# Gate tiles outside the ring, residual rows on GpSimd's queue, squares summed by additions, closing sums later

## The chip, the cores and the metric

The kernel runs on one core of one Trainium2 chip. The metric is the device time of one execution in microseconds (us); before the change the median of three executions is 1534.65 us.

## The reference

One decoder layer on x (256 positions x 2048 channels, float32), with 256 memory tokens:

```
x = x + hybrid_mixer(rms_norm(x, g1))          # w_in (five parts u, q, k, v, z and two logits per head), pooling, DeltaNet, w_mix_out
x = x + memory_cross_attention(rms_norm(x, g2), rms_norm(mem, gm))   # w_xq, w_xkv, w_xo
h = rms_norm(x, g3)
x = x + (silu(causal_dwconv(h @ w_gate) + b) * (h @ w_up)) @ w_down  # 2048 -> 5632 -> 2048
return rms_norm(x, g_final)
```

`rms_norm` multiplies by the reciprocal root of the mean square over the 2048 channels. Two of these norms matter here: the first (`rx`), whose squares are summed at the start, and the third (`r3`), whose sums close just before the gated MLP.

## The kernel before

Every weight is split into two float32r parts, a high part cast by ScalarE (ACT) and a low part, the difference, made by VectorE (DVE); a product is three matmuls on TensorE (PE): high by high, high by low, low by high. The programs of the engines are fixed when the kernel is built. Each engine runs its own in order, so an instruction that waits holds all that stand behind it on its engine; the DMAs that an engine issues stand in that same order.

**The start.** x arrives transposed. ACT squares it in four pieces of 128x1024 (L250) into `xsq`. The product with w_in runs head by head (`in_k`, casts and differences in lines 101 and 102). In between, `decays` works out the gates of the DeltaNet: `bc` and its transposes `lps`, then the sum of squares `xsum` by one TENSOR_REDUCE on DVE (L276, over the strided view of `xsq`), then `rnorm`, whose matmul `rxps` (L166) needs `xsum`, then a long chain of small DVE operations to `gg` (L304), the matmuls `gps` (L311) and the decay matmuls `dps` (L324).

**The gated MLP.** It begins where the last matmul of the cross-attention's output (`xo`, L141) ends. The gate and up weights are multiplied in 11 blocks of 22 steps, by a scheme of block sums and differences (seven products instead of eight). `plan` lists the steps: 11 kinds (`11`, `22`, `p1`, `s3`, `s1`, `p2`, `s2`, `21`, `p0`, `p3`, `s4`) of two tiles each, a tile being 128x1024. `load` (L987) fetches a tile 12 steps before its product, on SyncE's (SP's) queue; `prepare` splits it 4 steps before its product, and issues on GpSimd's (POOL's) queue the DMAs that add another weight onto a tile (L993) for the kinds built from sums. A first-gate tile (`11`) lies in `ring`, which is one of three large tiles under the tag "big" and takes the place of the attention's output `oT`; other tiles lie in 8 places under the tag "wr". The ring's tile is read again and again: by its own product, as target of L993 and L999, and as the source for `s1`, `s2` and `s4`.

**Beside the first block** two further jobs run, pumped along with the matmuls. `rows_of_x` turns the residual back to rows: 8 pieces of four PE transposes each (`xtp`), an ACT copy into `xt` (two places under the tag "sg") and a DMA to memory (`xspill`, L899, on SP's queue). `last_row` closes the sums of the third norm (`r3ps`, L166) and scales its last part. `xtp` and `r3ps` share the two PSUM banks under the tag "t".

Of the kernel before, what the change touches and what calls it, by code (L numbers as in the profile page):

```python
# [10 lines left out]
F32 = mybir.dt.float32  # L11
F32R = mybir.dt.float32r
AF = mybir.ActivationFunctionType
ALU = mybir.AluOpType
AX = mybir.AxisListType
NOSYNC = mybir.DependencyInfo(mybir.DependencyClass.NoSync, mybir.DependencyReason.DATA)

P = 128
# [24 lines left out]
def hybrid_trunk(ctx, tc, a, out):  # L43
    nc = tc.nc
    act, dve, pool, pe = nc.scalar, nc.vector, nc.gpsimd, nc.tensor
# [12 lines left out]
    def ev(name, n=T):  # L58
        return per.tile([P, n], F32, name=name, tag="ev", bufs=4)
# [4 lines left out]
    def job(lane, gen):  # L64
        lanes.setdefault(lane, []).append(gen)
# [15 lines left out]
    def drain(lane):  # L81
        while lanes.get(lane):
            advance(lane)
# [11 lines left out]
    def cv(k):  # L95
        s, e = CST[k]
        return cst[:, s:e]
# [15 lines left out]
    last_split = [None]  # L113
# [84 lines left out]
    with tc.tile_pool(name="dn", bufs=1, reuse_waits="tile") as dn:  # L198
# [18 lines left out]
        xsq = big("xsq", [P, KT, T], F32)  # L217
# [30 lines left out]
                    first(ps0, kt, hi[:, kt % 8, :], lo[:, kt % 8, :])  # L248
        for c in range(4):
            act.activation(xsq[:, c * 4:c * 4 + 4], xraw[c // 2][:, (c % 2) * 4:(c % 2) * 4 + 4], AF.Square)  # L250
        xsum = ev("xsum")
        nc.sync.dma_start(cst, a["cst"])
        rx, rxb, rxrun = rnorm([xsum], "rx")

# [10 lines left out]
        def decays():  # L265
            bc = dn.tile([16, T], F32, name="bc", tag="xp", bufs=3)
            act.copy(bc, bps[0:16, T:])
            dve.tensor_tensor(bc, bps[0:16, :T], bc, ALU.add)
            yield
            lps = pss.tile([P, 512], F32, name="lps", tag="s")  # L270
            for t in range(2):
                pe.transpose(lps[:, t * 16:(t + 1) * 16], bc[:, t * P:(t + 1) * P], cv("ident")[0:16, 0:16])
            lg = dn.tile([P, 2, 16], F32, name="lg")
            act.copy(lg.rearrange("p t c -> p (t c)"), lps[:, 0:32])
            with tc.issue_after(last_split[0].ins):
                dve.tensor_reduce(xsum, xsq.rearrange("p k t -> p t k"), AX.X, ALU.add)  # L276
            next(rxrun)
            yield from rxrun
            for t in range(2):
                dve.tensor_scalar(lg[:, t, :], lg[:, t, :], rx[:, t:t + 1], None, ALU.mult)  # L280
            blog = lg[:, :, 0:8].rearrange("p t h -> p h t")
            alog = lg[:, :, 8:16].rearrange("p t h -> p h t")
            act.activation(beta, blog, AF.Exp, scale=-1.0)
            dve.tensor_scalar(beta, beta, 1.0, None, ALU.add)
            dve.reciprocal(beta, beta)
            ea = dn.tile([P, 8], F32, name="ea")
            act.activation(ea, pv("a_log"), AF.Exp)
            xs, ab, yy, s1, s2, pp, gg = (sm(n) for n in ("xs", "ab", "yy", "s1", "s2", "pp", "gg"))
            dve.tensor_tensor(xs, alog, pv("dt_bias").unsqueeze(2).to_broadcast([P, HEADS, 2]), ALU.add)
            dve.tensor_scalar(ab, xs, -1.0, None, ALU.mult)  # L290
            dve.tensor_tensor(ab, ab, xs, ALU.min)
            act.activation(yy, ab, AF.Exp)
            dve.tensor_scalar(s1, yy, 2.0, None, ALU.add)
            dve.reciprocal(s1, s1)
            dve.tensor_tensor(s1, s1, yy, ALU.mult)
            dve.tensor_tensor(s2, s1, s1, ALU.mult)
            dve.tensor_scalar(pp, s2, 1.0 / 19.0, None, ALU.mult)
            for k in range(8, 0, -1):
                dve.scalar_tensor_tensor(pp, pp, 1.0 / (2 * k + 1), s2, ALU.add, ALU.mult)
            dve.scalar_tensor_tensor(pp, pp, 1.0, s1, ALU.add, ALU.mult)  # L300
            dve.tensor_scalar(xs, xs, 0.0, None, ALU.max)
            dve.scalar_tensor_tensor(xs, pp, 2.0, xs, ALU.mult, ALU.add)
            dve.tensor_scalar(ea, ea, -1.0, None, ALU.mult)
            dve.tensor_tensor(gg, xs, ea.unsqueeze(2).to_broadcast([P, HEADS, 2]), ALU.mult)  # L304
            ggf = fl(gg)
            mgr = dn.tile([P, P], F32R, name="mgr", tag="ktok", bufs=1)
            act.copy(mgr, cv("mgt"))
            for _ in range(7):
                yield
            gps = pss.tile([P, 512], F32, name="gps", tag="s")  # L310
            pe.matmul(gps[:, 0:16], cv("mle"), ggf, start=True, stop=True)  # L311
            pe.matmul(gps[:, 16:32], cv("mgt"), ggf, start=True, stop=True)
            act.activation(eg.rearrange("p s h t -> p (s h t)"), gps[:, 0:32], AF.Exp)
            dve.tensor_scalar(negA, egc, -1.0, None, ALU.mult)
            for q in range(4):
                gm = dn.tile([P, 4, P], F32, name="gm", tag="sq", bufs=1)
                for i in range(4):
                    dve.tensor_scalar(gm[:, i, :], cv("mle"), ggf[:, q * 4 + i:q * 4 + i + 1], None, ALU.mult)
                gh, gl = (dn.tile([P, 4, P], F32R, name=n, tag="C", bufs=2) for n in ("gh", "gl"))
                split(gh, gl, gm)  # L320
                yield
                yield
                dps = psd.tile([P, 512], F32, name="dps", tag="d")
                pe.matmul(dps, mgr, gh.rearrange("p i c -> p (i c)"), start=True, stop=False)  # L324
                pe.matmul(dps, mgr, gl.rearrange("p i c -> p (i c)"), start=False, stop=True)
                last_exp[0] = act.activation(Dm[q], dps.rearrange("p (i c) -> p i c", i=4), AF.Exp)
                pool.tensor_tensor(Dm[q], Dm[q], cv("mle").unsqueeze(1).to_broadcast([P, 4, P]), ALU.mult)
# [560 lines left out]
    acts = {}  # L888

    def rows_of_x():  # L890
        for q in range(8):
            t, n = q % 2, q // 2
            yield
            tp = pm.tile([P, 512], F32, name="xtp", tag="t", bufs=2)
            for i in range(4):
                pe.transpose(tp[:, half(i)], xres[:, 4 * n + i, half(t)], cv("ident"))
            xt = fp.tile([P, 512], F32, name="xt", tag="sg", bufs=2)
            act.copy(xt, tp)
            nc.sync.dma_start(xspill[t, :, n * 512:(n + 1) * 512], xt)  # L899
            yield  # L900


    latest = {}

    def seq(i):
        e = i.ins.engine
        if e in latest:
            tc.add_manual_dep(i.ins, latest[e], NOSYNC, reason="in the order of the text")
        latest[e] = i.ins.name
        return i  # L910
# [39 lines left out]
    def last_row():  # L950
        squared(15, sq3[0], "xo")
        scaled_rows(fp.tile([P, 1, T], F32, name="h15", tag="sg", bufs=2), 15, 1)
        r3, _, run = rnorm(sq3, "r3", False)
        job("r", run)
        return r3

    def parts(src, put=lambda i: i):
# [20 lines left out]
    def load(b, kind, j):  # L978
        w = {"11": 0, "22": 2, "21": 3, "s3": 1}.get(kind, int(kind[1]) if kind[0] == "p" else None)
        if w is None:  # L980
            return
        if kind == "11":
            r = ring[:, 2 * (b % 2) + j].rearrange("p (i c) -> p i c", i=2)
        else:
            r = fp.tile([P, 2, 512], F32, name="wr", tag="wr", bufs=8)
        raws[b, kind, j] = r
        nc.sync.dma_start(r, a["w_gu"][b, j, :, w])  # L987
# [44 lines left out]

    AHEAD, LOADS = 4, 8
    STAGES = (4, 6, 7, 8, 10, 12, 13, 15, 17, 18, 19, 21, 24, 25)
    job("xr", rows_of_x())
    convs = {}
    for s in range(LOADS):
        load(*plan[s])
    for s in range(-AHEAD, len(plan)):
        if s + LOADS + AHEAD < len(plan) and s + AHEAD >= 0:  # L1040
            load(*plan[s + LOADS + AHEAD])
        if s == -AHEAD:
            for q in range(LOADS, LOADS + AHEAD):
                load(*plan[q])
        if s + AHEAD < len(plan):
            prepare(*plan[s + AHEAD])
        if s == 1 - AHEAD:
            tc.add_manual_dep(added.ins, less[-1].ins.name, NOSYNC, reason="the last row's sums behind the first parts")
            with tc.issue_after(cast[-1].ins):
                r3 = last_row()  # L1050
        if s < 0:
            continue
        b, k = s // NS, s % NS
        if s == 16:
            drain("r")
        if k == 1 and b:
            convs[b - 1] = finish_block(b - 1)
        for c in (b - 1, b - 2):
            if c in convs and k + NS * (b - 1 - c) in STAGES:
                next(convs[c])  # L1060
        combine(b, k)
        multiply(*plan[s])
    for _ in convs[NB - 2]:
        pass
    job("cv", finish_block(NB - 1))
    drain("xr")


    arow = big("arow", [P, head_b, 4, T], F32)
# [35 lines left out]
    for m, (k, c) in enumerate(steps):  # L1105
# [4 lines left out]
        n = blocks.index(k // 4)  # L1110
# [122 lines left out]
```

## Time and profile before

| | |
|---|---|
| Median of three executions | 1534.65 us (1532.35 to 1535.73) |
| The profiled execution | 1533.36 us |
| Its span | 1531.6 us |
| Mean granted clock of TensorE | 0.992 |
| PE busy | 1490.8 us, 97% of the span |
| DVE busy | 1099.3 us, 72% |
| ACT busy | 856.4 us, 56% |
| POOL busy | 221.5 us, 14% |
| DMA | 314.95 MB, mean 206 GB/s |

The span is what the profiler sees between the first and the last instruction; the execution's own time is 1.8 us more. PE's 1490.8 us leave 41 us in which it has nothing to do. A granted clock below 1 in a stretch means that TensorE ran part of it at 1.2 GHz instead of 2.4 GHz. In a view of waits, each row names the waiting engine and line, what ended the wait, its total, how often, and the longest. The line numbers of the changed kernel are 2 higher in the start and 7 or 8 higher in the MLP.

### The profile page before, as it was taken

The page shows a single profiled execution, that of the slowest core. Times are in us where ns is not written, and L with a number is a line of the kernel's source. Part 1 is how long each engine was busy: PE and PEld are TensorE (multiplying, and loading weights), DVE is VectorE, ACT ScalarE, POOL GpSimd, SP SyncE. Part 2 cuts the span into 40 slices and gives each one's busy share as a digit, 9 for nine tenths or more (in the row PEclk, how much of TensorE's full clock was granted, in tenths as well). Part 3 has the DMA queues.
Part 4 walks back from the last instruction along what each step waited for, and adds up shares of the span by engine and source line. Part 5 has one row for each costly group of instructions (what it writes and reads, how often), then busy time and mean ns, then how long its engine had stood idle before and what let it go on. Part 6 is the DMA issues. An engine that isn't in the chain of part 4 may idle for free.

```text
span 1531.6 us, 20542 instructions
## 1 busy us (share of the span) xinstructions
PE 1490.8 (97%) x7722; PEld 1261.1 (82%) x7722; DVE 1099.3 (72%) x1435; ACT 856.4 (56%) x1247; POOL 221.5 (14%) x237
## 2 busy tenths in 40 slices
PE   7899999999999999999988999999999999999997
PEld 4788889888888888998877888888888888888885
DVE  6978887676544676666756898898999998455445
ACT  5555656554444544555545666666666666444433
POOL 0442532441100121000320000000000000000000
PEclk9999999999999999999999999999999999999999
DMA  6445443457555555344539888888888879755651
GB/s 225 155 176 176 151 170 126 141 173 268 190 176 190 192 191 192 138 140 163 193 129 339 248 256 261 260 256 268 269 270 242 244 217 365 249 194 191 197 188 55
DMA packets 73715, 314.95 MB, mean 206 GB/s; under 512 B 12048, under 2 KB 12432, under 8 KB 57488
## 3 DMA queue, kind: packets, MB, share of 16 engines
q1 hardware_dynamic: 67136, 290.05, 54.1%
q0 software_dynamic: 6336, 23.07, 8.4%
q8 instruction: 60, 0.98, 0.2%
q10 hardware_dynamic: 144, 0.52, 0.1%
q14 instruction: 39, 0.32, 0.1%
HBM read 304.05 MB, written 9.57 MB: 205 GB/s over the span
## 4 chain that ended last, share of the span: by engine, by line
PE 82%; DVE 7%; DMA 4%; ACT 2%; POOL 2%; issue 1%; SPq 1%; POOLq 0%; ACTq 0%; DVEq 0%
PE b L882 9%; PE b L884 9%; PE b L883 9%; PE acc L1096 5%; PE acc L1095 5%; PE acc L1094 5%; PE xq L143 4%; PE xo L143 4%; PE mix L143 4%; PE kk L143 3%; PE pvs L691 2%; PE pvs L690 2%; PE pvs L689 2%; PE xq L144 2%; PE xo L144 2%; PE mix L144 2%
## 5 line engine op out<-in xcount | busy, mean ns | idle before, releaser
L960 ACT CAST wh<-wr 128x1024 fp32r<-128x1024 f32 x154 | 160.2, 1050 | 82.4 <-DVE wr L996 30.0
L961 DVE TENSOR_TENSOR wl<-wr,wh 128x1024 fp32r<-128x1024 f32 x154 | 185.2, 1219 | 27.1 <-ACT wh L960 26.0
L882 PE MATMUL b<-wh,hP 128*128 128x512 f32 x484 | 192.4, 398 | 8.0 <-ACT wh L960 5.5
L884 PE MATMUL b<-wh,hP 128*128 128x512 f32 x484 | 191.8, 397 | 0.0
L883 PE MATMUL b<-wl,hP 128*128 128x512 f32 x484 | 190.6, 394 | 1.0 <-DVE wl L961 1.0
L961 DVE TENSOR_TENSOR wl<-wd,wh 128x1024 fp32r<-128x1024 f32 x88 | 107.5, 1224 | 101.9 <-ACT wh L960 100.3
L960 ACT CAST wh<-wd 128x1024 fp32r<-128x1024 f32 x88 | 92.7, 1054 | 118.5 <-PE acc L1096 115.7
L961 DVE TENSOR_TENSOR wl<-ring,wh 128x1024 fp32r<-128x1024 f32 x88 | 106.5, 1220 | 31.9 <-ACT wh L960 31.8
L960 ACT CAST wh<-ring 128x1024 fp32r<-128x1024 f32 x88 | 91.5, 1051 | 63.5 <-PE b L884 24.8
L1094 PE MATMUL acc<-wh,aring 128*128 128x512 f32 x320 | 124.5, 389 | 0.0
L1095 PE MATMUL acc<-wl,aring 128*128 128x512 f32 x320 | 124.5, 389 | 0.0
L1096 PE MATMUL acc<-wh,aring 128*128 128x512 f32 x320 | 124.5, 389 | 0.0
L882 PEld LDWEIGHTS b<-wh,hP 128*128 128x128 f32 x484 | 91.9, 190 | 28.0 <-ACT wh L960 5.8
L102 DVE TENSOR_TENSOR wil<-wi,wih 128x1024 fp32r<-128x1024 f32 x78 | 100.3, 1293 | 16.1 <-ACT wih L101 15.8
L883 PEld LDWEIGHTS b<-wl,hP 128*128 128x128 f32 x484 | 91.9, 190 | 20.3 <-DVE wl L961 1.9
L884 PEld LDWEIGHTS b<-wh,hP 128*128 128x128 f32 x484 | 91.8, 190 | 18.8
L993 POOL DMA_DIRECT2D ring<-in_w_gu x44 | 38.5, 879 | 422.2 <-DVE sg L932 343.1
L101 ACT CAST wih<-wi 128x1024 fp32r<-128x1024 f32 x78 | 81.4, 1048 | 18.0 <-DMA wi<-in_w_in 6.3
L143 PE MATMUL xq<-h2T,wqh 128*128 128x512 f32 x240 | 84.9, 393 | 0.0
L143 PE MATMUL kk<-mT,wkh 128*128 128x512 f32 x240 | 84.4, 393 | 0.0
L143 PE MATMUL xo<-oT,woh 128*128 128x512 f32 x240 | 84.3, 392 | 0.0
L143 PE MATMUL mix<-yT,wmh 128*128 128x512 f32 x240 | 84.1, 392 | 0.0
(466 smaller groups left out, 3769.9 us busy)
## 6 DMA issues: line engine op xcount, KB each, us to landing
wr<-in_w_gu SPq DMA_DIRECT2D x156, 512.0 KB, 7.0
wd<-in_w_down SPq DMA_DIRECT2D x88, 512.0 KB, 4.8
wi<-in_w_in SPq DMA_DIRECT2D x39, 1024.0 KB, 5.0
ring<-in_w_gu POOLq DMA_DIRECT2D x44, 512.0 KB, 7.4
wk<-in_w_k SPq DMA_DIRECT2D x16, 1024.0 KB, 4.9
wv<-in_w_v SPq DMA_DIRECT2D x16, 1024.0 KB, 4.8
wm<-in_w_mix SPq DMA_DIRECT2D x16, 1024.0 KB, 4.9
wq<-in_w_xq SPq DMA_DIRECT2D x16, 1024.0 KB, 4.9
```

Source lines behind the costliest of these rows:

```text
L101: act.copy(hi, src)
L102: return dve.tensor_tensor(lo, src, hi.bitcast(F32), ALU.subtract)
L143: pe.matmul(ps, h, full, start=kk == 0, stop=False)
L144: i = pe.matmul(ps[:, T:], l, xt[:, 0, :], start=False, stop=False)
L882: pe.matmul(ps, xh, wh, start=first and i == 0, stop=False, skip_group_check=True)
L883: pe.matmul(ps, xh, wl, start=False, stop=False, skip_group_check=True)
L884: m = pe.matmul(ps, xl, wh, start=False, stop=last and i == 1, skip_group_check=True)
L960: cast[:] = [put(act.copy(h, src))]
L961: less[:] = [put(dve.tensor_tensor(l, src, h.bitcast(F32), ALU.subtract))]
L1094: pe.matmul(acc[t, n], ah, wh, start=first, stop=False)
L1095: pe.matmul(acc[t, n], ah, wl, start=False, stop=False)
L1096: return pe.matmul(acc[t, n], al, wh, start=False, stop=last)
```

## The change

Four parts:

1. The two `11` tiles of the first block go to the "wr" places; those of later blocks stay in the ring.
2. The 8 residual rows are copied to four places of a tile of their own (tag "ac"), leave by POOL's queue, and are advanced by a written step (`next(leaving)`) in steps 3 to 19 of block 0, no longer pumped.
3. The squares are summed by five additions, issued right behind the squares; the TENSOR_REDUCE is gone.
4. `last_row` yields six times more before it closes its sums.

```diff
             act.activation(xsq[:, c * 4:c * 4 + 4], xraw[c // 2][...], AF.Square)
+        for c in range(1, 4):
+            dve.tensor_tensor(xsq[:, 0:4], xsq[:, 0:4], xsq[:, 4 * c:4 * c + 4], ALU.add)
+        dve.tensor_tensor(xsq[:, 0:2], xsq[:, 0:2], xsq[:, 2:4], ALU.add)
         xsum = ev("xsum")
+        dve.tensor_tensor(xsum, xsq[:, 0], xsq[:, 1], ALU.add)
...
-            with tc.issue_after(last_split[0].ins):
-                dve.tensor_reduce(xsum, xsq.rearrange("p k t -> p t k"), AX.X, ALU.add)
...
     def rows_of_x():
+        rows = fp.tile([P, 4, 512], F32, name="xt", tag="ac", bufs=1)
         for q in range(8):
             t, n = q % 2, q // 2
             yield
             tp = pm.tile([P, 512], F32, name="xtp", tag="t", bufs=2)
             for i in range(4):
-                pe.transpose(tp[:, half(i)], xres[:, 4 * n + i, half(t)], cv("ident"))
-            xt = fp.tile([P, 512], F32, name="xt", tag="sg", bufs=2)
-            act.copy(xt, tp)
-            nc.sync.dma_start(xspill[t, :, n * 512:(n + 1) * 512], xt)
+                seq(pe.transpose(tp[:, half(i)], xres[:, 4 * n + i, half(t)], cv("ident")))
             yield
+            seq(act.copy(rows[:, q % 4], tp))
+            nc.gpsimd.dma_start(xspill[t, :, n * 512:(n + 1) * 512], rows[:, q % 4])
...
-        job("r", run)
+        def later():
+            for _ in range(6):
+                yield
+            yield from run
+
+        job("r", later())
...
-        if kind == "11":
+        if kind == "11" and b:
             r = ring[:, 2 * (b % 2) + j].rearrange("p (i c) -> p i c", i=2)
         else:
             r = fp.tile([P, 2, 512], F32, name="wr", tag="wr", bufs=8)
...
-    job("xr", rows_of_x())
+    leaving = rows_of_x()
...
+        if 3 <= s < 20:
+            next(leaving, None)
...
-    drain("xr")
```

At the start, DVE's program changes as follows, behind the products' first differences (`w0l`; `wil` are the differences of the weights in_w_in):

```order
 L106 SCALAR_TENSOR_TENSOR hT<-xraw,prm,hT 128x256 x8
 L102 TENSOR_TENSOR w0l<-w_79,w0h 128x1024
-L268 TENSOR_TENSOR bc<-bps,bc 16x256
-L102 TENSOR_TENSOR wil<-wi,wih 128x1024 x2
-L276 TENSOR_REDUCE xsum<-xsq 128x256
-L102 TENSOR_TENSOR wil<-wi,wih 128x1024
+L252 TENSOR_TENSOR xsq<-xsq 128x1024 x2
+L272 TENSOR_TENSOR bc<-bps,bc 16x256
+L252 TENSOR_TENSOR xsq<-xsq 128x1024
+L253 TENSOR_TENSOR xsq<-xsq 128x512
+L255 TENSOR_TENSOR xsum<-xsq 128x256
+L102 TENSOR_TENSOR wil<-wi,wih 128x1024 x4
```

The reduction stood between the second and the third difference; the additions now stand ahead of the first difference, two of them also ahead of `bc`.

On SP, the loads from the last one of the cross-attention (`wo`) on, before:

```order
L110 DMA wo<-in_w_xo 128x2048 x16
L987 DMA ring<-in_w_gu 128x1024 x2
L987 DMA wr<-in_w_gu 128x1024 x10
L899 DMA xspill<-xt 128x512
L987 DMA wr<-in_w_gu 128x1024 x2
L899 DMA xspill<-xt 128x512
L987 DMA wr<-in_w_gu 128x1024
L899 DMA xspill<-xt 128x512
L987 DMA wr<-in_w_gu 128x1024
```

and now:

```order
L110 DMA wo<-in_w_xo 128x2048 x16
L994 DMA wr<-in_w_gu 128x1024 x9
L994 DMA ring<-in_w_gu 128x1024
L994 DMA wr<-in_w_gu 128x1024 x5
L994 DMA ring<-in_w_gu 128x1024
L994 DMA wr<-in_w_gu 128x1024 x4
L994 DMA ring<-in_w_gu 128x1024
```

The ring no longer stands first: nine loads into "wr" places stand ahead of it, and the residual rows have left this queue.

On POOL, the same stretch before (`sq` are the squares of the third norm, `r3r` its reciprocal root):

```order
L716 TENSOR_TENSOR sq_6743<-sq_6743,xos 128x256 x7
L993 DMA ring<-in_w_gu 128x1024 x2
L716 TENSOR_TENSOR sq_6743<-sq_6743,xos 128x256
L172 TENSOR_TENSOR r3r<-r3ms,cst 128x2
L993 DMA ring<-in_w_gu 128x1024 x42
```

and now:

```order
L718 TENSOR_TENSOR sq_6747<-sq_6747,xos 128x256 x7
L1000 DMA wr<-in_w_gu 128x1024 x2
L718 TENSOR_TENSOR sq_6747<-sq_6747,xos 128x256
L902 DMA xspill<-xt 128x512
L172 TENSOR_TENSOR r3r<-r3ms,cst 128x2
L902 DMA xspill<-xt 128x512
L1000 DMA wr<-in_w_gu 128x1024 x2
L902 DMA xspill<-xt 128x512 x5
L1000 DMA ring<-in_w_gu 128x1024
L902 DMA xspill<-xt 128x512
L1000 DMA ring<-in_w_gu 128x1024 x39
```

The eight rows now stand among the accumulating DMAs: two ahead of the second pair, seven ahead of the first one for block 1, all eight ahead of the next.

## Rows read from the trace of the kernel before

**Rows 1.** TensorE's waits in the whole span: engine, line, releaser, total, times, longest.

```profile
PE b L882 <- ACT wh L960: 5.5, 1, 5.5
PE dps L324 <- ACT gh L101: 2.7, 3, 1.8
...
PE b L882 <- DVE ring L1019: 2.5, 1, 2.5
PE gps L311 <- DVE gg L304: 1.9, 1, 1.9
...
PE xtp L896 <- ACT xt L898: 1.7, 1, 1.7
PE in_k L144 <- DVE wil L102: 1.2, 2, 0.8
...
PE rxps L166 <- DVE xsum L276: 0.8, 1, 0.8
```

**Rows 2.** Busy us of each engine, granted clock, DMA share and GB/s by stretch.

```profile
35.00:39.00 4.00, 4.00 (x16) 3.41 (x15) 2.64 (x3) 0.48 (x1) 0.93 (x1) 0.60 0.61 199
60.00:72.00 12.00, 10.13 (x53) 7.96 (x52) 12.00 (x23) 6.47 (x11) 7.62 (x7) 1.00 0.46 164
773.00:791.00 18.00, 18.00 (x106) 15.81 (x105) 8.67 (x12) 6.34 (x11) 3.48 (x3) 1.00 0.00 1
791.00:797.00 6.00, 0.50 (x4) 0.19 (x2) 0.13 (x1) 1.04 (x1) 0.00 (x0) 0.91 0.71 237
797.00:803.00 6.00, 5.53 (x13) 3.70 (x13) 5.28 (x6) 4.88 (x7) 3.03 (x3) 0.52 0.99 357
803.00:808.00 5.00, 3.81 (x21) 2.95 (x20) 3.92 (x4) 2.40 (x5) 0.00 (x0) 1.00 1.04 283
808.00:852.00 44.00, 40.58 (x183) 32.82 (x184) 29.24 (x28) 25.22 (x31) 5.13 (x5) 0.96 1.02 350
852.00:900.00 48.00, 48.00 (x221) 39.66 (x220) 42.48 (x46) 32.69 (x39) 3.46 (x4) 1.00 0.83 235
900.00:1200.00 300.00, 300.00 (x1378) 246.84 (x1376) 270.88 (x296) 198.44 (x232) 24.39 (x28) 1.00 0.87 258
1240.00:1500.00 260.00, 260.00 (x1164) 215.09 (x1163) 152.95 (x145) 124.38 (x130) 1.74 (x2) 1.00 0.67 223
```

**Rows 3.** DVE's timeline at the start: start, us, engine, line, what, [idle before].

```profile
16.64 1.22 DVE L102 TENSOR_TENSOR w0l<-w,w0h 128x1024 fp32r<-128x1024 f32 x1
19.93 0.41 DVE L268 TENSOR_TENSOR bc<-bps,bc 16x256 f32<-16x256 f32 x1 [2.07 <-ACT bc L267]
23.32 2.36 DVE L102 TENSOR_TENSOR wil<-wi,wih 128x1024 fp32r<-128x1024 f32 x2 [2.98 <-ACT wih L101]
25.59 7.44 DVE L276 TENSOR_REDUCE xsum<-xsq 128x256 f32<-128x4096 f32 x1
32.94 1.22 DVE L102 TENSOR_TENSOR wil<-wi,wih 128x1024 fp32r<-128x1024 f32 x1
```

**Rows 4.** Of the tile ring's instructions: durations min/median/max in ns, first and last start.

```profile
L1019 DVE TENSOR_TENSOR ring<-q,b x11: 686/686/689, 838.3 to 1266.9; 128x512 f32<-128x512 f32 x11
...
L993 POOL DMA_DIRECT2D ring<-in_w_gu x44: 857/868/1060, 798.7 to 1259.7; - x44
```

**Rows 5.** SP's queue's waits for xo and for the rows' copies, 785 to 900 us.

```profile
SPq L987 <- PE xo L141: 25.0, 1, 25.0
SPq L899 <- ACT xt L898: 14.5, 6, 3.3
```

**Rows 6.** DVE's timeline ahead of the MLP: the last two parts of hP.

```profile
772.13 1.23 DVE L102 TENSOR_TENSOR hP<-hc,hP 128x1024 fp32r<-128x1024 f32 x1 [0.57 <-ACT hP L101]
...
788.56 0.96 DVE L102 TENSOR_TENSOR hP<-hc,hP 128x768 fp32r<-128x768 f32 x1 [1.81 <-ACT hP L101]
```

**Rows 7.** ACT's timeline at the first cast of the MLP.

```profile
795.79 1.04 ACT L960 CAST wh<-ring 128x1024 fp32r<-128x1024 f32 x1 [7.26 <-DMA ring<-in_w_gu]
```

**Rows 8.** ACT's waits for the residual rows' landing, 785 to 860 us.

```profile
ACT xt L898 <- DMA xspill<-xt: 8.8, 5, 2.7
```

## The prediction

> **What bounds the kernel now.** I read the shares of the span first: TensorE is busy for 1490.8 of 1531.6 us, so no more than about 41 us can be had without taking matmuls away, and this change, which takes none away, can only act on TensorE's pauses and on its clock. So I read next TensorE's own waits over the whole span [rows 1], to see where the pauses lie, and then the busy time, clock and DMA share by stretch [rows 2], to see what is around them. Two places belong to this change. At the start (20 to 75 us) TensorE waits for xsum, for a difference (wil), for gg and for gh, in sum 6.6 us [rows 1], and between 35 and 39 us it works at a granted clock of 0.60 [rows 2]. At the beginning of the MLP (791 to 852 us) it waits 5.5 us for the first cast, 1.7 us at the row transposes and 2.5 us for a combination in DVE [rows 1], and its clock is 0.52 from 797 to 803 us [rows 2]. Behind 852 us it is busy for all of 48, 300 and 260 us in the three stretches shown [rows 2]: what is won before that is not lost to a wait that is there already, and reaches the end unless loads, casts or differences fall behind.
>
> **The squares.** Removed: one reduction of 7.44 us on DVE, which starts at 25.59 [rows 3]. Added: three additions of 128x1024 at 1.22 us (a difference of that shape, the row of 16.64), one of 128x512 at 0.69 [rows 4] and one of 128x256 at 0.41 (the addition of bc, which has as many elements in a lane) [rows 3]: 3 x 1.22 + 0.69 + 0.41 = 4.76 us. They stand ahead of the first difference, where DVE is idle for 2.07 us ahead of bc and 2.98 us behind it, 5.05 us in all [rows 3]. So I cost them at nothing; what hides them are DVE's waits for bc and for the cast of wih. If that cover were gone they would cost 4.76 us, still 2.7 less than the reduction. xsum is then there near 22.7 us instead of 33.0, and the third difference, at 32.94 behind the reduction, follows the first two at once.
>
> What TensorE gets of it. (a) 0.8 us of waiting for xsum and about 0.4 of the wil row's 1.2 (its longest wait, 0.8, lies ahead of the reduction and stays). (b) The low clock of 35 to 39 us follows that pause; work at a granted share of 0.60 for 4.00 us loses 4.00 x 0.40 = 1.6 us [rows 2]. (c) The waits for gg (1.9) and gh (2.7) [rows 1] end a chain on DVE that starts from the norm's factor, and so from xsum. That chain starts some 7 us earlier, but on an engine that is full: 12.00 of 12 us from 60 to 72 [rows 2]. Bounds: nothing of (c), since DVE's work is not less by more than 7.44 - 4.76 us and TensorE comes earlier too, against all 4.6 us. The additions lie in idle time, so DVE's own row moves up by the full 7.44 while TensorE moves up by 2.8; that is nearer to the upper end, and I take 3.2. Sum of the start: 0.8 + 0.4 + 1.6 + 3.2 = 6.0 us, with ends at 2.8 and 7.4.
>
> **First gate tiles.** Before, SP's first MLP load waits for the last matmul of xo, 25.0 us [rows 5], since the ring takes the place of oT; everything behind it on that queue waits too. From 773 to 791 us the DMA engines are idle (share 0.00, 1 GB/s) [rows 2]. The first cast starts at 795.79, after 7.26 us in which ACT waited for that tile [rows 7]. Now nine loads into "wr" places stand ahead of the ring's first. By the places' former users the first seven need nothing later than the part of hP of 772.13, which ends at 773.4; the eighth needs the last part, 788.56 to 789.5 [rows 6]. So seven tiles (7 x 0.524 = 3.67 MB) come between 773 and 791, in idle DMA time, and the first casts and differences follow ACT's and DVE's last work for hP, before TensorE ends xo at 791.4. TensorE does not stop, and with the pause its low clock goes.
>
> What is there to be won, by stretch [rows 2]: idle 5.50 + 0.47 + 1.19 + 3.42 = 10.6 us from 791 to 852 us, and lost to the clock 5.53 x 0.48 + 40.58 x 0.04 = 2.65 + 1.62 = 4.3 us: 14.9 us, the upper end.
>
> What limits it is the DMA. From 797 to 852 us its share is 0.99 to 1.04 [rows 2]. The bytes from 791 to 852 are 6 x 237 + 6 x 357 + 5 x 283 + 44 x 350 kB = 20.4 MB, and the 55 full us move 345 GB/s. Take away the 3.67 MB that now come early, let the rest start at 789.5 with the eighth load, and the same point of the program is reached at 789.5 + 16.7 / 0.345 = 837.9 at the full rate, and at 839.8 if only the last xo matmul releases the bulk. That is 14.1 or 12.2 us before 852. I take 12.5, near the second, since two pauses can remain inside: the transposes wait for an ACT copy that stands behind casts (1.7 now, [rows 1]), and the combination in DVE that TensorE waited 2.5 us for stands where it stood. With both of them kept and coming on top it would be 12.2 - 4.2 = 8.0, the lower end.
>
> **Rows and closing sums.** The eight row DMAs leave SP's queue, where they stood between loads, and ACT's 8.8 us of waiting for their landing [rows 8] goes with the four places. They are issued by POOL at the price of a DMA there, 0.87 us (857 to 1060 ns) [rows 4]: 8 x 0.87 = 7.0 us on an engine that is busy for 5.1 of 44 us [rows 2]. Each stands ahead of accumulating DMAs and holds these until its ACT copy is done. I cost this at nothing beyond the two pauses above; what hides it is that an accumulation is issued four steps ahead of its product, and a step is (61 - 15) / 22 = 2.1 us of TensorE, so 8 us of cover. Without the cover, all 7.0 us would show. The bytes are the same, so the sum of the DMA stands. The later closing sums take matmuls from behind step 3 to behind step 5 and wait for POOL's last square no longer; nothing needs their result before the scaling of step 16: nothing either way.
>
> *A rule against this part.* The row's issues on POOL took at most 1060 ns, though DVE was busy for 270.88 of the 300 us in which most of them fall. The Trainium skill, "DMA: Bandwidth & Descriptors", section "SWDGE vs HWDGE vs iDMA", advises plain transfers on SP or ACT, since descriptors that GpSimd writes are held up by some of DVE's instructions; "SBUF — State Buffer", section "A bandwidth-pool intuition that's wrong", gives some 3100 ns where 620 was normal, a factor of 5. By the row the rows cost 7.0 us of hidden issue time; by the rule 35, which would not be hidden.
>
> **Sum.** -6.0 - 12.5 = -18.5 us on the profiled execution's 1533.4: 1514.9. The median of the runs shown is 1.3 above the profiled one, so 1516 us.
>
> **Rivals.**
> - *The start gives back.* DVE, full from 60 to 72 us, sets the start whatever TensorE does, and only the MLP pays, with nothing to 2.8 us from the start: 1534.65 - 12.5 - 1.4 = 1521 us. For it: the 12.00 of 12. Against it: 7.44 us leave DVE itself.
> - *The early tiles gain little.* If the loads of 773 us wait after all for something late, or the DMA is what counts and the bulk starts at 791.4 as before, then 20.4 MB / 0.345 = 59 us end at 850.5: 2 us of gain instead of 12.5, and with the start 1534.65 - 2 - 6 = 1527 us. For it: DMA shares of 1.0 up to 852. Against it: idle DMA from 773 on, and a wait [rows 5] that names xo alone.
> - *POOL's queue holds up the sums (slower).* The row issues stand in order with the accumulations, seven of them ahead of block 1's first, and each waits for its ACT copy, as SP did at most 3.3 us for one [rows 5]. If these waits don't lie beside each other, a row takes 0.87 + 3.3 = 4.2 us of the queue, the accumulation behind all eight comes 33.4 us later, 8 are covered, and TensorE stops for 25.4 us in block 1 and restarts at the low clock (2.65, as at 797 us): 1516 + 28 = 1544 us, slower than before. Up to 1.0 us a row it does nothing; the kernel is as slow as before from 3.0 us a row (24 - 8 + 2.65 = 18.65). Against it: a row comes only every second step, 4.2 us, so POOL is done with one before the next, and the longest of 44 issues took 1.06 us. (By the Trainium skill's factor, above, the issue alone would take 4.35 us, beyond the point from which this decides; the trace's 1.06 speaks against it.)
>
> **How the numbers follow.** A measurement of this kernel can tell about 0.2%, 3 us, from no change. Forecast with both gains 0.64 (own range 1510 to 1521); start given back 0.12; early tiles gain little 0.12; POOL's queue 0.05; the remaining 0.07 for what no row shows, half of it near no change. Faster takes the first three less a little: 0.87; same 0.06; slower 0.07. The range reaches from the upper ends of both sums (1534.65 - 7.4 - 14.9 = 1512, less 2 for what a profile's spread can hide, 1510) to the second rival's 1527.
>
> **What would show it.** In the profile after: no reduction on DVE, TensorE's wait for xsum gone and the clock near 1.0 from 30 to 39 us; waits for gg and gh below 2 us in sum; loads landing from 773 us on; the first MLP product within 1 us of the last xo matmul, at full clock; no wait for a landing at the copies of the rows; POOL's row issues near 0.9 us; TensorE's idle time over 791 to 840 us below 3 us. The forecast is wrong if TensorE stops again between steps 3 and 21 for an accumulation or a load, or if the DMA's full stretch ends no earlier than before.

## The result and the profile after

The changed kernel takes 1518.61 us (median of four executions, 1517.98 to 1519.94); its ratio to the kernel before is 0.9899, 95% interval 0.9881 to 0.9916, so 15.5 us less (12.9 to 18.3). The forecast was 1516, its range 1510 to 1527. The profiled execution took 1517.98 us, with a span of 1516.2.

TensorE's waits over the whole span of the changed kernel, to be set beside [rows 1] (engine, line, releaser, total, times, longest):

```profile
PE gps L313 <- DVE gg L306: 3.0, 1, 3.0
PE dps L326 <- ACT gh L101: 2.8, 2, 2.5
PE xtp L899 <- ACT xt L901: 2.4, 2, 1.5
...
PE in_k L143 <- ACT wih L101: 1.4, 1, 1.4
PE b L884 <- DVE ring L1026: 1.1, 1, 1.1
PE in_k L144 <- DVE wil L102: 0.8, 1, 0.8
```

The 5.5 us for the first cast of the MLP are gone, and so is the wait for xsum. But gg is now waited for 3.0 us instead of 1.9, and gh 2.8 instead of 2.7. The stretches of [rows 2], after (busy us of each engine, granted clock, DMA share, GB/s):

```profile
35.00:39.00 4.00, 4.00 (x23) 3.15 (x22) 3.77 (x11) 1.80 (x5) 1.39 (x1) 1.00 0.51 215
48.00:60.00 12.00, 10.47 (x51) 9.07 (x52) 10.22 (x23) 6.27 (x11) 4.14 (x4) 0.86 0.25 89
60.00:72.00 12.00, 9.14 (x44) 7.10 (x44) 10.84 (x20) 6.58 (x11) 6.93 (x7) 0.94 0.34 107
72.00:80.00 8.00, 8.00 (x47) 7.16 (x46) 6.01 (x8) 6.98 (x16) 4.05 (x6) 0.87 0.61 233
773.00:791.00 18.00, 18.00 (x100) 15.60 (x99) 10.39 (x13) 9.94 (x14) 5.36 (x6) 1.00 0.65 213
791.00:797.00 6.00, 6.00 (x30) 4.99 (x29) 5.84 (x6) 3.23 (x5) 0.00 (x0) 1.00 1.01 260
797.00:803.00 6.00, 4.50 (x25) 3.77 (x25) 3.91 (x5) 3.12 (x5) 1.32 (x2) 1.00 0.78 271
803.00:808.00 5.00, 4.08 (x22) 3.09 (x21) 3.16 (x3) 2.93 (x4) 0.05 (x1) 1.00 0.97 338
808.00:852.00 44.00, 42.89 (x202) 35.02 (x201) 34.45 (x33) 28.81 (x36) 7.47 (x11) 1.00 0.94 313
852.00:900.00 48.00, 48.00 (x221) 39.57 (x221) 43.92 (x50) 32.46 (x38) 4.36 (x5) 1.00 0.89 259
```

The low clock of 35 to 39 us is gone, but two others have come, from 50 to 54 and from 71 to 74 us, behind the waits for gg and gh. From 773 to 900 us the clock is 1.00 in all the stretches, and 10.6 us of idle time have become 3.5 (1.50 + 0.92 + 1.11; the prediction's sign asked for less than 3). On SP the first nine loads are issued from 769 us on (seven by 773 us, the eighth at 785, the ninth at 792), and ACT's first casts of the MLP stand directly behind its part of hP of 128x768; first SP's timeline, then ACT's:

```profile
769.03 23.70 SPq L994 DMA_DIRECT2D wr<-in_w_gu  x9
```

```profile
783.28 0.83 ACT L101 CAST hP<-hc 128x768 fp32r<-128x768 f32 x1
784.02 3.90 ACT L967 CAST wh<-wr 128x1024 fp32r<-128x1024 f32 x4
```

**Two marks.** From the traces I take two times of each kernel: the start of TensorE's last xo matmul (what lies before it is the start's gain), and the time from there to the first transpose of the gate, gt (22 steps of block 0 and the first of block 1; in every kernel the same number of matmuls). Before: 791.0 and 66.8 us. After: 786.6 and 54.9 us. So in this pair of profiles 4.4 us come from ahead of the MLP and 11.9 from its beginning; behind gt both kernels take nearly the same, 422 us to the down projection's first matmul and 241 to 242 from there to its last; the changed one loses 0.9 us there, all in all, which makes the 15.4 us between the two spans.

| kernel | last xo | xo to gt | timed median | ratio to before (95%) |
|---|---|---|---|---|
| before | 791.0 | 66.8 | 1534.7 | 1 |
| changed | 786.6 | 54.9 | 1518.6 | 0.9899 (0.9881 to 0.9916) |
| changed, again | 788.7 | 53.1 | 1519.3 | 0.9904 (0.9884 to 0.9924) |
| additions alone | 788.2 | 66.7 | 1533.5 | 0.9998 (0.9988 to 1.0008) |
| gate tiles alone | 793.0 | 66.8 | 1531.5 | 0.9981 (0.9970 to 0.9993) |
| changed, old rows | 788.7 | 66.8 | 1529.2 | 0.9973 (0.9962 to 0.9983) |
| changed, tiles in the ring | 789.7 | 64.0 | 1527.9 | 0.9958 (0.9942 to 0.9973) |
| changed, two places | 788.6 | 64.1 | 1527.3 | 0.9956 (0.9939 to 0.9972) |
| changed, rows pumped | 786.9 | 61.8 | 1524.7 | 0.9935 (0.9915 to 0.9955) |
| changed, with the reduction | 791.8 | 52.5 | 1521.8 | 0.9921 (0.9905 to 0.9937) |
| changed, sums not later | 788.4 | 54.0 | 1519.7 | 0.9910 (0.9891 to 0.9928) |
| changed, rows on SP | 787.5 | 52.3 | 1516.7 | 0.9889 (0.9875 to 0.9904) |
| the same, no double load | 787.9 | 52.4 | 1517.6 | 0.9889 (0.9873 to 0.9905) |
| changed, gps later | 794.0 | 52.4 | 1521.8 | 0.9925 (0.9910 to 0.9940) |

The first two columns are of one profiled execution each, the others of the timed ones; I compare kernels by their ratios, since each ratio is taken to the kernel before as it ran beside it.

### The profile page after: what moved, and what is told of

Its sections match the earlier page's. It is cut to its first block, busy times and chain, and to the rows that moved or that the text cites. A ratio compares the mean times of both kernels' runs of the same rounds, so it can differ in the third digit from the quotient of the medians.

```text
span 1516.2 us, 20536 instructions
## 1 busy us (share of the span) xinstructions
PE 1483.5 (98%) x7722; PEld 1257.2 (83%) x7722; DVE 1097.7 (72%) x1439; ACT 856.9 (57%) x1247; POOL 224.7 (15%) x245
## 4 chain that ended last, share of the span: by engine, by line
PE 82%; DVE 6%; DMA 4%; ACT 3%; POOL 2%; issue 2%; SPq 0%; DVEq 0%; POOLq 0%; ACTq 0%
PE b L884 9%; PE b L886 9%; PE b L885 9%; PE acc L1102 5%; PE acc L1103 5%; PE acc L1104 5%; PE xq L143 4%; PE mix L143 4%; PE xo L143 3%; PE kk L143 3%; PE pvs L693 2%; PE pvs L692 2%; PE pvs L691 2%; PE xq L144 2%; PE mix L144 2%
## 5 line engine op out<-in xcount | busy, mean ns | idle before, releaser
L967 ACT CAST wh<-wr 128x1024 fp32r<-128x1024 f32 x162 | 168.4, 1050 | 90.8 <-PE b L886 32.0
L968 DVE TENSOR_TENSOR wl<-wr,wh 128x1024 fp32r<-128x1024 f32 x162 | 194.8, 1219 | 29.4 <-ACT wh L967 28.0
L967 ACT CAST wh<-ring 128x1024 fp32r<-128x1024 f32 x80 | 83.2, 1051 | 52.8 <-PE b L886 26.9
L968 DVE TENSOR_TENSOR wl<-ring,wh 128x1024 fp32r<-128x1024 f32 x80 | 96.7, 1218 | 20.1 <-ACT wh L967 20.1
L1000 POOL DMA_DIRECT2D ring<-in_w_gu x40 | 34.9, 872 | 378.8 <-DVE sg L934 350.8
```

What stands on the lines that cost most here:

```text
L967: cast[:] = [put(act.copy(h, src))]
L968: less[:] = [put(dve.tensor_tensor(l, src, h.bitcast(F32), ALU.subtract))]
```

## The experiments

**The additions alone**, in the kernel before:

```diff
+        for c in range(1, 4):
+            dve.tensor_tensor(xsq[:, 0:4], xsq[:, 0:4], xsq[:, 4 * c:4 * c + 4], ALU.add)
+        dve.tensor_tensor(xsq[:, 0:2], xsq[:, 0:2], xsq[:, 2:4], ALU.add)
+        dve.tensor_tensor(xsum, xsq[:, 0], xsq[:, 1], ALU.add)
-                dve.tensor_reduce(xsum, xsq.rearrange("p k t -> p t k"), AX.X, ALU.add)
```

> The kernel before with the additions alone in place of the reduction. Theory: all that the start gives comes from the additions; of the 5.2 us that TensorE is ahead at the end of its fourth unit (42.11 instead of 47.32 us) 4.4 are lost again at gps, which now stands 12 matmuls earlier and waits 2.98 us for gg, with a stretch at 1.2 GHz behind it; 0.8 us are left at 78 us, and 3.2 more come between 140 and 160 us, where the stretch at 1.2 GHz at 154 us is gone: 1534.7 - 4.0 = 1530.7 us, the same waits for gg (about 3.0) and gh (about 2.8) as in the changed kernel. Rival: the 3.2 us at 150 us belong to the chance of one execution, not to the additions: 1533.8 us. Second rival: without the MLP's part the start keeps its 6.0 us, as predicted: 1528.7 us.

Measured: 1533.46 us, ratio 0.9998; 0.3 us less, at most 1.8. The first rival's time came nearest, 1533.8; the theory's 4.0 us and the predicted 6.0 are excluded by the interval. The waits are those of the theory, though (gg 3.0, gh 2.6), and this kernel's profile has its last xo matmul 2.8 us earlier than before. That profiled execution was the shortest of the ten, 1530.5 us.

**The reduction back**, in the changed kernel (the additions out, the TENSOR_REDUCE in):

```diff
-        for c in range(1, 4):
-            dve.tensor_tensor(xsq[:, 0:4], xsq[:, 0:4], xsq[:, 4 * c:4 * c + 4], ALU.add)
...
+                dve.tensor_reduce(xsum, xsq.rearrange("p k t -> p t k"), AX.X, ALU.add)
```

> The changed kernel with the single reduction of the squares back in place of the additions. Theory: the additions give nothing that lasts, since gps and dps come earlier and wait longer (alone they gave 0.5 us, interval -1.2 to 1.8): within 1.5 us of the changed kernel, in whose first 80 us the reduction's wait (0.8) and the stretch at 1.2 GHz near 35 us come back and the wait for gg falls from 3.0 to 1.9. Rival: the profiles are right, by which the additions put TensorE 2 to 4 us ahead behind 160 us: 2 to 4 us more than the changed kernel.

Measured: ratio 0.9921 against 0.9904 of the changed kernel beside it, 2.6 us more: the rival's size (2 to 4), not the theory's (within 1.5), but with intervals that overlap. One stretch of its start shows the old picture again:

```profile
31.00:39.00 8.00, 6.86 (x23) 5.95 (x24) 5.49 (x7) 1.09 (x2) 1.61 (x1) 0.57 0.49 166
```

All ten profiles with the additions and gps in its place have the last xo matmul between 786.6 and 789.7 us, the three without them between 791.0 and 793.0. So profiles say some 3 to 4 us, the timed runs 0.3 to 2.6. What part of the 15.5 us the additions give stays open between 0 and 4; none of these numbers reaches the 6.0 of the prediction.

**gps later**, in the changed kernel:

```diff
-            for _ in range(7):
+            for _ in range(9):
                 yield
             gps = pss.tile([P, 512], F32, name="gps", tag="s")
```

> The changed kernel with nine yields instead of seven ahead of gps, which puts gps 9 matmuls later on TensorE and the four dps pairs 9, 15, 19 and 20 matmuls later. Theory: the start gave back its gain because gps and dps stand too early for DVE's chain; now gps waits about 1.5 us instead of 3.0, the last dps not at all instead of 2.5, and at least one of the two stretches at 1.2 GHz (50.1 and 70.6 us, 1.7 us each) goes: 4 to 6 us less, 1512.6 to 1514.6 us. Rival: DVE's chain sets the pace there, the waits only move on to qp and w behind 140 us: 1518.6 us, within 1 us, with the wait for Z longer than 1.6 us.

Measured: 1521.78 us, ratio 0.9925, slower by 3 to 4 us than the changed kernel (the intervals just overlap). TensorE's waits of this kernel, whole span:

```profile
PE qp L425 <- DVE Z L420: 5.7, 2, 5.4
...
PE gps L313 <- DVE gg L306: 1.5, 1, 1.5
```

The wait for gg is halved and the one for gh gone, and the last matmul of the product's eighth unit (a unit is one head's 16 steps) starts at 72.5 us instead of 76.9. But the wait for Z, behind 140 us, grows from 1.6 to 5.7 us, and the last xo matmul starts at 794.0. The theory was wrong. The rival had the mechanism, that the waits only move on to where DVE's chain ends; its time, within 1 us of the changed kernel, was too low. The four dps pairs started 0.6 to 3.4 us later here, and they feed the DeltaNet's chain of DVE, ACT and POOL that ends in Z; that this lateness made the longer wait fits, but no run isolates it.

**The gate tiles alone**, in the kernel before:

```diff
-        if kind == "11":
+        if kind == "11" and b:
             r = ring[:, 2 * (b % 2) + j].rearrange("p (i c) -> p i c", i=2)
```

> The kernel before with the first gate tiles outside the ring alone; rows on SP's queue, two places, reduction and early closing sums as before. Theory: what this part gives by itself is the pause and the low clock at the MLP's start, 5.5 + 0.5 + 2.65 = 8.7 us, and the waits at the transposes (1.7) and for the combination in DVE (2.5, with 1.6 of low clock) stay: 1526 us. Rival: the DMA decides, so that the seven early tiles give the whole 11.8 us that the MLP's stretch gained: 1522.9 us. Second rival: the rows on SP's queue and ACT's waits for their landing give most of it back: 1530 us or more.

Measured: 1531.53 us, ratio 0.9981, 2.9 us less (1.1 to 4.6). In the profile the first product starts 0.23 us behind the start of the last xo matmul instead of 5.9, and yet gt comes 66.8 us after it, as before. The second rival was right. ACT's longest group of waits from 785 to 860 us in this kernel, against 8.8 in [rows 8], TensorE's waits at the transposes, against 1.7 in [rows 1], and its stretch from 808 to 838 us:

```profile
ACT xt L898 <- DMA xspill<-xt: 17.1, 4, 8.3
```

```profile
PE xtp L896 <- ACT xt L898: 4.7, 3, 3.8
```

```profile
808.00:838.00 30.00, 23.86 (x102) 18.60 (x101) 12.01 (x11) 12.57 (x16) 1.79 (x2) 0.90 0.87 259
```

TensorE started earlier and waited for the rows instead. (The profiled execution was the longest of ten, 1536.0 us; by their median something of the gain stays.)

**The old rows**, in the changed kernel (its second part undone):

```diff
-        rows = fp.tile([P, 4, 512], F32, name="xt", tag="ac", bufs=1)
+            xt = fp.tile([P, 512], F32, name="xt", tag="sg", bufs=2)
+            act.copy(xt, tp)
+            nc.sync.dma_start(xspill[t, :, n * 512:(n + 1) * 512], xt)
...
+    job("xr", rows_of_x())
```

> The changed kernel with its whole second part undone: rows pumped along with the matmuls, two places under the tag sg, SP's queue; gate tiles, additions and later closing sums stay. Theory: the gate tiles pay in full only when the rows no longer hold ACT, whose copies waited for the landing of an earlier row and let TensorE wait for casts (alone the gate tiles gave 2.4 us, with 6.1 of 30 us idle from 808 to 838 us): 1529 to 1531 us, 10 to 12 more than the changed kernel. Rival: what was missing beside the gate tiles were the later closing sums, which left the transposes one bank of two: 1519 to 1522 us.

Measured: 1529.23 us, ratio 0.9973, 10.6 us slower than the changed kernel; the theory's time. The later closing sums are in this kernel, so they were not what was missing. Of the chain of waits from 799 to 832 us in it (start, us, what), the larger pieces behind 801 us:

```profile
801.18 8.94 DMA xspill<-xt
...
815.82 4.78 DMA xspill<-xt
820.70 0.60 ACT xt L900
821.31 9.42 DMA xspill<-xt
...
831.31 1.06 ACT wh L967
```

23.1 of these 30 us are three landings of rows. With two places, a copy waits on ACT until the row two before it has landed; the cast behind the copy waits with it, and TensorE waits for the copy (4.1 us at the transposes in this kernel) or for what the cast begins. The kernel before has the same chain at the same place:

```profile
808.43 8.27 DMA xspill<-xt
816.80 0.60 ACT xt L898
817.41 4.94 DMA xspill<-xt
822.45 0.59 ACT xt L898
...
825.60 7.35 DMA xspill<-xt
833.53 1.06 ACT wh L960
```

**Tiles in the ring again**, in the changed kernel:

```diff
-        if kind == "11" and b:
+        if kind == "11":
```

> The changed kernel with the first gate tiles back in the ring; rows, additions and later closing sums stay. From TensorE's last xo matmul to the first transpose of the gate (gt) the kernel before takes 66.8 us, the changed one 53 to 55; with the gate tiles but the old rows it is 66.7 and 66.8. Theory: the stretch goes by the later of two chains, the rows' (copy, landing, copy) and the loads'; with the rows' chain gone, the pause of 5.9 us and the low clock (2.65) of the ring come out again: 60 to 62 us for the stretch, 1525 to 1528 us. Rival: the rows' part alone makes the whole gain, the gate tiles are worth nothing: 53 to 55 us, 1519 to 1520 us.

Measured: 1527.89 us, ratio 0.9958; 8.3 us slower than the changed kernel by the ratios. The time is the theory's; the stretch, 64.0 us, is longer than the 60 to 62 expected. TensorE's two longest waits from 780 to 860 us in it:

```profile
PE b L884 <- ACT wh L967: 5.4, 1, 5.4
...
PE xtp L899 <- ACT xt L901: 3.3, 1, 3.3
```

The pause of [rows 1] is back, and with it the clock of 1.2 GHz: from 793 to 800 us, and again from 814 to 817. So the rows' part without the gate tiles, together with the additions and the later sums, gives 6.4 us of the 15.5.

**Two places**, in the changed kernel:

```diff
-        rows = fp.tile([P, 4, 512], F32, name="xt", tag="ac", bufs=1)
+        rows = fp.tile([P, 2, 512], F32, name="xt", tag="ac", bufs=1)
-            seq(act.copy(rows[:, q % 4], tp))
+            seq(act.copy(rows[:, q % 2], tp))
```

> The changed kernel with two places for the residual rows instead of four; written steps and POOL's queue stay. Theory: with two places each copy waits for the landing of the row two before it (some 8 us), which holds the casts behind it on ACT: the stretch from xo to gt is back at 64 to 67 us, 1528 to 1531 us. Rival: what counts is that the rows go by written steps instead of being pumped: 53 to 56 us, 1519 to 1521 us.

Measured: ratio 0.9956, 8.0 us slower than the changed kernel; 64.1 us from xo to gt, within the theory's 64 to 67; the time, 1527.25 us, is just under its 1528. ACT waits for a landing again, and TensorE at the transposes for ACT's copies:

```profile
ACT xt L901 <- DMA xspill<-xt: 9.7, 2, 9.3
```

```profile
PE xtp L899 <- ACT xt L901: 8.6, 2, 7.1
```

**Pumped rows**, with four places and POOL's queue:

```diff
-    leaving = rows_of_x()
+    job("xr", rows_of_x())
-        if 3 <= s < 20:
-            next(leaving, None)
```

> The changed kernel with the residual rows pumped along with the matmuls as before, but with four places and on POOL's queue. Theory: the places count, not the steps; four rows can be on their way at once: 53 to 57 us from xo to gt, 1519 to 1522 us. Rival: pumped rows come so close to each other that ACT waits for landings all the same: 62 us or more, 1527 us or more.

Measured: ratio 0.9935, 4.8 us slower than the changed kernel, 61.8 us from xo to gt: between theory and rival, and for neither's reason. ACT does not wait for a row's landing. The rows come faster (all eight copies between 795.2 and 818.0 us instead of 799.5 and 831.8), and TensorE's long wait is for the combination in DVE:

```profile
PE b L884 <- DVE ring L1026: 4.9, 1, 4.9
```

With that pause the clock falls to 1.2 GHz, from 825 to 835 us. ACT waited 13.4 us for weight tiles meanwhile, against 6.4 in the changed kernel. So the written steps count too; probably because they spread the 2.1 MB of rows over more of the loads' time, which no run isolates.

**Sums not later**, in the changed kernel:

```diff
-            for _ in range(6):
-                yield
             yield from run
```

> The changed kernel without the six yields, so that the closing sums come as early as before. Theory: nothing needs them before step 16, they change little: within 2 us of the changed kernel. Rival: they hold one of the two banks between the row transposes, and wait for POOL's last square, so TensorE stops again: 3 to 5 us more, with a wait of r3ps for the squares.

Measured: 1519.70 us, ratio 0.9910, within 1 us of the changed kernel (0.9904): the theory. The wait of r3ps for the squares is there (1.3 us), but the 3 to 5 us of the rival are not.

**The rows on SP's queue**, in the changed kernel:

```diff
-            nc.gpsimd.dma_start(xspill[t, :, n * 512:(n + 1) * 512], rows[:, q % 4])
+            nc.sync.dma_start(xspill[t, :, n * 512:(n + 1) * 512], rows[:, q % 4])
```

> The changed kernel with the residual rows issued on SP's queue again, still with four places and written steps. Theory: the queue that the rows leave by matters little, the gate tiles did the work: 1518.6 us within 1.5, with TensorE's idle time from 791 to 840 us near the 3.5 of now. Rival: on SP each row holds the loads behind it until its ACT copy (14.5 us in six waits before), and TensorE waits for casts again: 4 to 6 us more, 1523 to 1525 us.

Measured: 1516.71 us, ratio 0.9889, no slower than the changed kernel, if anything faster by 1.5 to 2.3 us (the intervals overlap). With four places and written steps the queue makes no difference that these runs can tell. The Trainium skill, "DMA: Bandwidth & Descriptors", section "SWDGE vs HWDGE vs iDMA", would have plain transfers on SP or ACT; the direction of this run agrees, its size is within what the runs spread.

**No double load**, with the rows on SP:

```diff
-        if s + LOADS + AHEAD < len(plan) and s + AHEAD >= 0:
+        if s + LOADS + AHEAD < len(plan) and s >= 0:
```

> The changed kernel with the rows on SP's queue (ratio 0.9889 to the kernel before) and without a second load of the two p2 tiles of the first block, which the kernel before and the changed one both issue twice (158 loads into wr places become 156). Theory: with the rows' chain gone the MLP's beginning hangs on the loads (the chain of waits of the changed kernel lies for 42% of 786 to 842 us in loads, the DMA share is 1.03); 1.05 MB less at 345 GB/s are 3.0 us: 1513 to 1515 us, ratio 0.987, below both kernels. Rival: the loads have room, TensorE idles for only 1.5 us there: 1516.7 us, ratio 0.9889, within 1 us.

Measured: 1517.56 us, ratio 0.9889, the same as with the rows on SP and the double load: the rival. From 808 to 838 us TensorE has no pause left to lose:

```profile
808.00:838.00 30.00, 30.00 (x144) 24.86 (x143) 21.05 (x21) 19.71 (x25) 3.51 (x4) 1.00 1.04 346
```

So the DMA, at a share of 1.04, does not hold TensorE there. No version run is clearly faster than the changed kernel.

**The changed kernel again**, for comparison:

> The changed kernel itself, as the measure for the three beside it: 1518.6 us within 1.5, ratio to the kernel before 0.990.

Measured: 1519.29 us (1514.78 to 1523.90), ratio 0.9904.

## Why the prediction was right, and where it was not

**The time** was right to 2.6 us, in part by luck: a term that was too large (6.0 us for the start, where 0 to 4 came) stood beside one that by the timed runs was a little small (12.5 us, where some 13 to 15 of the 15.5 came from the MLP). The time alone does not choose between the forecast and the rival that gives the start back: 1518.6 lies 2.6 us from 1516 and 2.4 from 1521.

**The squares: cover right, gain wrong.** DVE's timeline at the start, to be set beside [rows 3]:

```profile
17.27 2.54 DVE L252 TENSOR_TENSOR xsq<-xsq 128x1024 f32<-128x1024 f32 x2
19.73 0.40 DVE L272 TENSOR_TENSOR bc<-bps,bc 16x256 f32<-16x256 f32 x1
20.06 1.20 DVE L252 TENSOR_TENSOR xsq<-xsq 128x1024 f32<-128x1024 f32 x1
21.30 0.69 DVE L253 TENSOR_TENSOR xsq<-xsq 128x512 f32<-128x512 f32 x1
22.03 0.42 DVE L255 TENSOR_TENSOR xsum<-xsq 128x256 f32<-128x256 f32 x1
22.88 2.36 DVE L102 TENSOR_TENSOR wil<-wi,wih 128x1024 fp32r<-128x1024 f32 x2 [0.42 <-ACT wih L101]
```

The additions cost what was worked out (4.85 us by these rows), lie in the idle time, and xsum is there at 22.45 us. Terms (a) and (b) came: no wait for xsum, 0.8 us left at wil as said, clock 1.00 from 35 to 39 us. Term (c), 3.2 us for gg and gh, is the step that failed. DVE's chain did come earlier: gps ran at 49.5 instead of 55.8 us, 6.3 us. But gps itself stands 12 matmuls earlier in TensorE's program, as rxps stands 11 earlier, and TensorE was 5.2 us ahead at the last matmul of the fourth unit (42.1 against 47.3). I counted DVE's gain without this new place. The waits for gg and gh stayed at 5.8 us in sum instead of falling below 2, and two stretches at 1.2 GHz followed them. At the last matmul of the eighth unit 0.8 us were left (76.9 against 77.7). "DVE's own row moves up by the full 7.44 while TensorE moves up by 2.8" was the wrong sentence; the rival that gives the start back was the right one for this part.

Not all that the pair of profiles shows at the start belongs to the additions. Of the 5.2 us, 0.8 were there at the end of the first unit, and some 1.5 are a stretch at 1.2 GHz in the kernel before that the prediction did not name:

```profile
24.00:28.00 4.00, 3.40 (x11) 2.93 (x12) 4.00 (x3) 2.22 (x3) 0.00 (x0) 0.57 0.90 328
```

Three profiles with the additions have it too (two places, no double load, gps later), so it does not hang on the reduction. The 0.8 us that were left at the eighth unit become 4.1 between 140 and 195 us, where the wait for Z is 1.6 us instead of 2.5 and the profile before has a stretch at 1.2 GHz, at 154 us, that the one after lacks; four others with the additions have one there, between 150 and 155 us.

**Gate tiles: right in mechanism, not alone.** Loads from 769 us on, the first product 0.23 us behind xo, full clock: all as said. The size came to 11.9 and 13.7 us in the two profiles for the 12.5 forecast. But the working gave all of it to this part. By the timed ratios the gate tiles are worth 2.9 us alone and 8.3 beside the new rows.

**The rows "at nothing": the step that was wrong.** The prediction put what their part costs at nothing, and gave it no gain of its own. Their four places and written steps are what the gate tiles' gain needs: without them 10.6 us are lost, with two places 8.0, with pumping 4.8. The mistake was in the reading: I took TensorE's waits [rows 1], of which only 1.7 us name the rows, and saw ACT's 8.8 us for their landing [rows 8] as time off the path, though the chain of waits of the kernel before, shown above, puts 20.6 us of the stretch into three landings. Once TensorE starts earlier, ACT's wait for the landings doubles to 17 us and takes the gain.

**The DMA as the limit: not shown.** The 3.67 MB that were to come early did (18 x 213 kB = 3.8 MB from 773 to 791 us). But that the 12.5 taken from the DMA's rate agreed was, as far as the runs show, chance: the kernel with the rows on SP passes the stretch in 52.3 us with 1.5 us of pause, at the same shares, and there 1.05 MB less changed nothing. So some 51 us of the stretch are TensorE's own work, and of the 66.8 before no more than 16 could be had, whatever the DMA does. (In the changed kernel itself, with its 3.5 us of pause, fewer bytes were not tried.)

**The rival on POOL's queue** was wrong as weighed: the row issues took 539 to 902 ns, below the 0.87 us of the working in the median, and TensorE's waits name no accumulation. The issues and landings of the rows in the changed kernel:

```profile
L902 POOL DMA_DIRECT2D xspill<-xt x8: 539/572/902, 800.4 to 832.7; - x8
```

POOL did wait for the copies, 29.3 us in six, without harm that the runs show. **The closing sums** changed nothing, as said.

## What to carry to other kernels

When a wait is taken away at the head of a stretch, follow the chain of waits through the rest of that stretch before giving it the gain: a buffer that comes free only when a store has landed can set the end without showing up as a long wait of the bottleneck engine. Where two such chains lie side by side, removing one gives less than it seems to promise, and removing both more than the sum (here 2.9 us for the gate tiles alone, 6.4 for all but the gate tiles, 15.5 for everything). And where an instruction's place is counted from an event that moves, a gain moves the instruction that waits as well; putting it later helps only if nothing hangs on its result.

## What was not expected of the hardware

A row of 256 KB needed up to 13.0 us to land beside the loads, 9.0 in the median (6.8 before), though its issue takes well under 1 us: with the DMA at a share of 0.94 to 1.04, a store's buffer was held some fifteen times as long as its issue. And profiles and timed runs disagreed on the additions (3 to 4 us against 0.3 to 2.6), and one profile does not stand for all executions: the changed kernel's six of one series lay between 1514.8 and 1523.9 us.
